# Another model of the chip behind the order of each engine's instructions, in a two-block transformer kernel

## The chip, the cores and the metric

The kernel runs on one core of one Trainium2 chip. The metric is the time of one execution on the device in microseconds (us), as the median of several runs; the other times here come from one execution that the hardware profiler recorded.

## The reference, cut to what matters

The reference is one stack of three layers on a sequence of 512 positions with 1024 features. Everything is computed in 32-bit floats.

```python
def reference(x, ...):
    x = first_block(x, ...)             # attention, HGRN2, RWKV-7 and RG-LRU side by side, then an MLP
    return second_block(x, c_2, ctx_2, ...)   # two layers, with a context of 256 rows

# first_block
h = rms_norm(x, norm_mix_pre)
pa, pb, pc, pd = split(h @ w_in)
mix = concat([chunk_attention(pa), hgrn2(pb), rwkv7(pc), rglru(pd)])
x = x + rms_norm(mix @ w_out, norm_mix_post)
x = x + rms_norm(square(relu(rms_norm(x) @ mlp_w1)) @ mlp_w2, norm_mlp_post)

# second_block, layer l of 2
mx = silu(c) @ ada_w[l] + ada_b[l]       # shifts, scales and gates
hx = rmsnorm(x) * (1 + scale) + shift    # the same for the context rows
yx = mixer_ab(hx, hc) if l == 0 else mixer_mla(hx, hc)   # window + differential / latent attention
x = x + gate * rmsnorm(yx)
x = x + gate * rmsnorm(swiglu(modulated x, ffn_w13[l], ffn_w2[l]))
```

## The kernel before

Every large product is made in three passes of TensorE (`mm3`, L203 to L209): each operand is kept as a high and a low part of a reduced float type, and high x high, low x high and high x low are added in one PSUM bank. A weight comes from HBM into `wr` (L186 and L183, three buffers, from SyncE's queue), ScalarE makes its high part `wh` (L199) and VectorE its low part `wl` (L200), two buffers each. An accumulated bank is emptied by VectorE or ScalarE, in the last products of a block by `out_last` (L1101, the sum at L1115).

The program is one straight line without loops at run time. It is written with Python generators: `weave` (L241) takes one step of a main generator and then, by a share written as a number (`W`, L1864, and `STEP`, L2068), steps of others, so that matmuls of one part stand between the dependent steps of another. In the first block the steps of RWKV (L527 to L592), of HGRN2 (L795 to L870) and of attention are woven with projections and with the `ada` products (L1016, the matmuls at L1028, two buffers of 1024 KB for their tile `aw`, loads at L1026). In layer 0 of the second block a unit of attention computes its scores while the one before it is weighted (`unit`, in `mixer0`, L2075); layer 1 does the same for latent attention (`Mla`, L1553). Between blocks stands a chain for each pair of 128-row tiles (`Post`, L1802): a product with a gain row (L1825 on GpSimd, L1826 on VectorE), a sum of squares (ScalarE, L1848), a power on GpSimd (L1852), the residual (L1829), the same norm again with L1837 at its end, and transposes on TensorE (L1754 in `two_to_F`) whose results become the next block's operands.

The order of the program is not the order of the engines. When the context of the kernel closes, a scheduler goes through all instructions with a model of the chip: at each moment of the model's time an engine gets, among the instructions whose inputs and buffers the model holds to be ready, the one that stands first in the program. What comes out is one fixed list for each engine, with semaphore waits, and the engines work through their lists.

## Time and profile before

| | us |
|---|---|
| median of 3 runs | 2566.88 |
| lowest, highest | 2566.58, 2567.56 |
| the profiled execution | 2560.58 |
| its span, first to last instruction | 2558.5 |
| TensorE busy in it | 2440.3 |
| VectorE, ScalarE, GpSimd busy | 1203.4, 995.0, 303.7 |

The profiled execution is 6.3 us shorter than the median. A matmul counts as busy from its start to a modelled end, so a row of matmuls without a hole is busy all the time, whatever their pace. In the rows below PE is TensorE's matmuls and PEld its weight loads, DVE is VectorE, ACT ScalarE, POOL GpSimd and SPq the queue of SyncE; L12 is line 12 of the kernel. PEclk is the granted share of TensorE's full clock.

### The profile page before, as it was taken

The page shows a single profiled execution, that of the slowest core. Times are in us where ns is not written, and L with a number is a line of the kernel's source. Part 1 is how long each engine was busy: PE and PEld are TensorE (multiplying, and loading weights), DVE is VectorE, ACT ScalarE, POOL GpSimd, SP SyncE. Part 2 cuts the span into 40 slices and gives each one's busy share as a digit, 9 for nine tenths or more (in the row PEclk, how much of TensorE's full clock was granted, in tenths as well). Part 3 has the DMA queues.
Part 4 walks back from the last instruction along what each step waited for, and adds up shares of the span by engine and source line. Part 5 has one row for each costly group of instructions (what it writes and reads, how often), then busy time and mean ns, then how long its engine had stood idle before and what let it go on. Part 6 is the DMA issues. An engine that isn't in the chain of part 4 may idle for free. (4 is left out here: it accounts for less than half of the span.)

```text
span 2558.5 us, 37902 instructions
## 1 busy us (share of the span) xinstructions
PE 2440.3 (95%) x15436; PEld 1976.2 (77%) x15436; DVE 1203.4 (47%) x2075; ACT 995.0 (39%) x1802; POOL 303.7 (12%) x393
## 2 busy tenths in 40 slices
PE   8999989999999989989899999999899999999998
PEld 6567747888888867767888888888776667888886
DVE  5644464433446575773531232333656663523334
ACT  4742234332235454653522221212555554432222
POOL 0101132000001122320200000000222221000001
PEclk9999999999999999999999999999999999999999
DMA  8754575333334312122412222222321123333332
GB/s 267 258 197 163 167 267 167 91 91 99 93 105 139 85 45 66 56 84 83 148 58 66 59 66 66 73 68 71 112 60 35 40 66 117 114 93 97 99 107 91
DMA packets 251005, 270.74 MB, mean 106 GB/s; under 512 B 23744, under 2 KB 198256, under 8 KB 244688
## 3 DMA queue, kind: packets, MB, share of 16 engines
q1 hardware_dynamic: 249600, 264.00, 33.4%
q0 software_dynamic: 1232, 4.33, 0.5%
q8 instruction: 121, 1.98, 0.3%
q14 instruction: 52, 0.43, 0.0%
HBM read 231.90 MB, written 25.45 MB: 101 GB/s over the span
## 5 line engine op out<-in xcount | busy, mean ns | idle before, releaser
L207 PE MATMUL ps<-hFh,wh 128*128 128x512 f32 (+1 forms) x1752 | 628.8, 360 | 7.8 <-ACT qk_l L1273 2.5
L208 PE MATMUL ps<-hFl,wh 128*128 128x512 f32 (+1 forms) x1752 | 624.9, 357 | 1.8 <-DVE hFl L266 1.6
L209 PE MATMUL ps<-hFh,wl 128*128 128x512 f32 (+1 forms) x1752 | 623.3, 356 | 0.5 <-DVE wl L200 0.5
L200 DVE TENSOR_TENSOR wl<-wr,wh 128x1024 fp32r<-128x1024 f32 (+3 forms) x258 | 307.0, 1191 | 651.5 <-ACT wh L199 649.5
L199 ACT CAST wh<-wr 128x1024 fp32r<-128x1024 f32 (+3 forms) x258 | 263.1, 1021 | 704.2 <-PE ps L208 346.5
L207 PEld LDWEIGHTS ps<-hFh,wh 128*128 128x128 f32 x1752 | 333.4, 191 | 72.9 <-issue 12.1
L209 PEld LDWEIGHTS ps<-hFh,wl 128*128 128x128 f32 x1752 | 333.4, 191 | 52.0 <-issue 4.3
L208 PEld LDWEIGHTS ps<-hFl,wh 128*128 128x128 f32 x1752 | 333.8, 191 | 48.9 <-DVE hFl L266 3.2
L207 PE MATMUL ps<-wh,h_h 128*128 128x512 f32 x590 | 229.7, 389 | 0.6 <-ACT wh L199 0.6
L208 PE MATMUL ps<-wl,h_h 128*128 128x512 f32 x590 | 229.7, 389 | 0.0
L209 PE MATMUL ps<-wh,h_l 128*128 128x512 f32 x590 | 229.5, 389 | 0.0
L1825 POOL TENSOR_TENSOR yg<-y,gainrow 128x512 f32<-128x512 f32 x28 | 38.7, 1384 | 1319.6 <-DVE y L1115 866.7
L207 PEld LDWEIGHTS ps<-wh,h_h 128*128 128x128 f32 x590 | 110.8, 188 | 24.0 <-ACT wh L199 1.1
L208 PEld LDWEIGHTS ps<-wl,h_h 128*128 128x128 f32 x590 | 110.8, 188 | 22.9 <-DVE wl L200 0.2
L209 PEld LDWEIGHTS ps<-wh,h_l 128*128 128x128 f32 x590 | 110.8, 188 | 23.0
L1234 DVE TENSOR_TENSOR hraw<-hraw,ps 128x512 f32<-128x512 f32 (+1 forms) x70 | 40.1, 573 | 174.4 <-PE ps L209 174.4
L265 ACT CAST h_h<-hraw 128x512 fp32r<-128x512 f32 (+1 forms) x70 | 36.9, 527 | 120.9 <-DVE hraw L1234 120.9
L208 PE MATMUL ps<-wl,hFh 128*128 128x256 f32 (+2 forms) x256 | 80.3, 314 | 0.2 <-DVE wl L200 0.2
L207 PE MATMUL ps<-wh,hFh 128*128 128x256 f32 (+2 forms) x256 | 80.4, 316 | 0.1
L209 PE MATMUL ps<-wh,hFl 128*128 128x256 f32 (+2 forms) x256 | 80.0, 312 | 0.0
L1626 DVE TENSOR_REDUCE sm<-ps 128x1 f32<-128x768 f32 x64 | 60.8, 954 | 37.4 <-PE ps L209 36.2
L1630 POOL TENSOR_SCALAR ms<-ms,sm 128x768 f32<-128x768 f32 x64 | 60.2, 943 | 150.2 <-DVE sm L1629 145.3
(643 smaller groups left out, 4197.9 us busy)
## 6 DMA issues: line engine op xcount, KB each, us to landing
wr<-in_ffn_w_dram SPq DMA_DIRECT2D x126, 512.0 KB, 3.9
aw<-in_ada_w_dram SPq DMA_DIRECT2D x48, 1024.0 KB, 5.1
wr<-in_mlp_w_dram SPq DMA_DIRECT2D x60, 512.0 KB, 4.0
wr<-in_w_in_dram SPq DMA_DIRECT2D x25, 512.0 KB, 6.7
x<-xr SPq DMA_DIRECT2D x20, 512.0 KB, 3.0
xr<-x SPq DMA_DIRECT2D x18, 512.0 KB, 4.4
wr<-in_ab_w_in_dram SPq DMA_DIRECT2D x16, 512.0 KB, 5.0
wr<-in_w_out_dram SPq DMA_DIRECT2D x8, 512.0 KB
```

The source lines that it names most:

```text
L199: nc.scalar.copy(dst(hi), view(raw))
L200: nc.vector.tensor_tensor(out=dst(lo), in0=view(raw), in1=dst(hi).bitcast(F32), op=SUB)
L207: mm(out, a.hi, b.hi, start=start, stop=False)
L208: mm(out, a.hi, b.lo, start=False, stop=False)
L209: mm(out, a.lo, b.hi, start=False, stop=stop)
L265: nc.scalar.copy(s.hi, x)
L1234: v.tensor_tensor(out=raw[:, c], in0=raw[:, c], in1=p, op=MUL)
L1626: v.tensor_reduce(out=mx, in_=p[:, 0:768], axis=AX.X, op=MAX, negate=True)
L1630: nc.gpsimd.tensor_scalar(out=s, in0=s, scalar1=r, scalar2=1.0, op0=MUL, op1=MUL)
L1825: nc.gpsimd.tensor_tensor(out=t[:, h[0]], in0=y[:, h[0]], in1=g[:, h[0]], op=MUL)
```

## The change

The scheduler gets another model of the chip: a model made of timelines in place of the one that executes the program. The one line in `kernel`:

```diff
-    with tile.TileContext(nc) as tc, ExitStack() as es:
+    with tile.TileContext(nc, schedule_with_timeline_sim=True) as tc, ExitStack() as es:
         network(make(tc, I, es), out[0])
```

The instructions, the tiles and the order of the program stay as they are. The five lists, of TensorE, VectorE, ScalarE, GpSimd and SyncE, are made anew, and with them the waits and the buffers that each tile gets.

## Rows read from the trace of the kernel before

**Rows 1.** The page's busy time by engine, and the core's span and clock.
```profile
PE 2440.3 (95%) x15436; PEld 1976.2 (77%) x15436; DVE 1203.4 (47%) x2075; ACT 995.0 (39%) x1802; POOL 303.7 (12%) x393
...
core 0: 2558.5 us, clock 0.984
```
**Rows 2.** Busy us in stretches: PE, PEld, DVE, ACT, POOL; PEclk, DMA share, GB/s.
```profile
0.00:64.00 64.00, 52.14 (x280) 41.12 (x280) 32.29 (x84) 28.52 (x44) 6.06 (x26) 1.00 0.85 267
...
128.00:192.00 64.00, 61.62 (x880) 44.23 (x879) 30.74 (x41) 27.07 (x39) 0.44 (x1) 0.97 0.59 197
192.00:256.00 64.00, 62.55 (x1028) 49.13 (x1028) 30.55 (x51) 16.17 (x26) 7.33 (x4) 1.00 0.50 163
256.00:320.00 64.00, 61.41 (x993) 47.41 (x991) 31.46 (x62) 16.89 (x28) 7.97 (x7) 1.00 0.51 167
320.00:384.00 64.00, 53.93 (x652) 32.12 (x651) 43.00 (x121) 24.99 (x58) 21.70 (x26) 0.95 0.77 267
...
512.00:576.00 64.00, 64.00 (x280) 52.12 (x279) 22.60 (x24) 23.53 (x32) 0.00 (x0) 1.00 0.32 91
...
896.00:960.00 64.00, 56.46 (x313) 42.98 (x310) 45.67 (x100) 35.47 (x74) 17.65 (x27) 0.94 0.17 45
960.00:1024.00 64.00, 59.19 (x361) 48.03 (x362) 35.12 (x99) 29.59 (x69) 16.69 (x29) 0.93 0.23 65
1024.00:1088.00 64.00, 60.53 (x383) 47.71 (x382) 47.89 (x121) 39.40 (x87) 20.63 (x34) 1.00 0.19 58
1088.00:1152.00 64.00, 53.36 (x293) 39.31 (x291) 44.92 (x111) 35.75 (x75) 18.41 (x30) 0.92 0.27 82
...
1856.00:1920.00 64.00, 57.96 (x342) 47.35 (x340) 38.30 (x70) 37.32 (x76) 19.06 (x24) 0.97 0.26 59
1920.00:1984.00 64.00, 62.97 (x386) 44.06 (x385) 39.35 (x66) 34.52 (x70) 17.54 (x18) 1.00 0.14 35
1984.00:2048.00 64.00, 61.93 (x378) 44.13 (x378) 38.85 (x65) 34.22 (x69) 16.60 (x17) 1.00 0.15 41
2048.00:2112.00 64.00, 61.44 (x361) 42.30 (x359) 42.57 (x70) 37.68 (x73) 17.23 (x17) 1.00 0.21 65
...
2496.00:2558.00 62.00, 53.39 (x233) 43.14 (x232) 26.71 (x40) 15.52 (x30) 7.36 (x8) 0.96 0.29 94
```
**Rows 3.** Instructions from 362 to 373: start, duration, what; brackets: idle before, releaser.
```profile
368.93 0.69 DVE L866 TENSOR_TENSOR f<-ps,hsm 128x512 f32<-128x512 f32 x1 [1.54 <-POOL hsm L864]
...
369.68 1.15 PE L869 MATMUL ps<-c_masks,f 64*64 64x64 f32 x32 [1.95 <-DVE f L866]
...
370.76 1.06 PE L1028 MATMUL ps<-aw,sc 128*32 128x512 f32 x8
```
**Rows 4.** The DMA issues of SyncE from 340 to 373, the last two ada loads.
```profile
360.90 5.83 SPq L1026 DMA_DIRECT2D aw<-in_ada_w_dram  x2
```
**Rows 5.** The page's DMA issues: count, KB each, median us from issue to landing.
```profile
aw<-in_ada_w_dram SPq DMA_DIRECT2D x48, 1024.0 KB, 5.1
...
wr<-in_w_in_dram SPq DMA_DIRECT2D x25, 512.0 KB, 6.7
```
**Rows 6.** Instructions from 1784 to 1800, columns as in rows 3.
```profile
1790.86 0.60 PE L1754 MATMUL ps<-c_ident,y 128*128 128x128 f32 x4
...
1792.23 0.68 DVE L1115 TENSOR_TENSOR y<-y,ps 128x512 f32<-128x512 f32 x1
...
1794.85 0.75 DVE L1837 TENSOR_SCALAR y<-xr,sm 128x1024 f32<-128x1024 f32 x1 [1.47 <-POOL sm L1852]
...
1795.74 2.79 PE L1754 MATMUL ps<-c_ident,y 128*128 128x128 f32 x12 [4.29 <-DVE y L1837]
...
1798.19 0.73 PE L207 MATMUL ps<-h_h,h_h 128*128 128x512 f32 x1
```
**Rows 7.** What TensorE waited for in total: us, times, longest us.
```profile
PE ps L1754 <- DVE y L1837: 13.6, 6, 4.3
```
**Rows 8.** Busy us behind the wait of rows 6, columns as in rows 2.
```profile
1795.00:1800.00 5.00, 4.25 (x19) 3.98 (x20) 4.34 (x9) 3.42 (x7) 0.54 (x1) 0.66 0.38 105
```

## What is to be expected of the change

> **What bounds the kernel now.** I read the granted clock first, then the head of the page, then the busy time of each engine in forty stretches of 64 us, then what TensorE waited for, then the order of single instructions around two of its waits. TensorE is busy for 2440.3 of 2558.5 us, no other engine for half of that [rows 1]. So the kernel is bound by its matmuls, and 118.2 us is all the time in which TensorE does nothing. The change leaves the number and the shapes of the matmuls as they are, so it can only win from these 118.2 us and from the slower clock: the mean granted clock is 0.984 [rows 1], and 1.6% of the span, 41 us, is what that costs at most.
>
> The stretches are of three kinds [rows 2]. In 14 of the 40 (896 us: the MLP and the two FFNs; one row stands for all) TensorE is busy for 64.00 of 64 us. Nothing can be won there. The first stretch has 11.9 us of idle time and the last 8.6 us; both are loads and norms with no other work to do. What is left, 97.7 us, lies in the woven stretches, where the chained steps of one generator are filled with the matmuls of another, and at the boundaries between blocks. The woven ones are 128 to 320 (RWKV steps), 896 to 1152 (window and differential attention) and 1856 to 2112 (latent attention): 11 rows, 704 us, of which TensorE does 185.58 + 229.54 + 244.30 = 659.42 us. In 320 to 384, where a chain has little left to be filled with, it is busy for 53.93 of 64 us, a share of 0.843.
>
> **What the change does, part by part.** It adds and removes no instruction, no tile and no DMA. For each engine the scheduler takes the instructions by the moment at which its model of the chip holds them to be ready, and by their place in the program among those that are. The model is exchanged, so the orders on TensorE, VectorE, ScalarE, GpSimd and in SyncE's DMA queue may all move. The model's own run is before the launch and costs nothing in these times. Four effects count.
>
> *Stalls with ready work behind them (a gain).* At 367.7 the matmul at the head of the queue (L869) waits for VectorE (L866), which itself waits for a GpSimd step (L864), and TensorE stands for 1.95 us. Behind it, at 370.76, are eight ada matmuls that need none of this: their tile's load was issued at 360.90 [rows 3, 4], and with the median of 5.1 us to landing [rows 5] it was there at 366.0. They would have put 1.06 us into the hole. At 1790.86 four transposes run, then TensorE waits 4.29 us for a normalised row (L1837), with twelve more transposes first in the queue. The projection matmuls behind those (L207 at 1798.19) begin a new accumulation, and the bank for it is one that L1115 empties at 1792.23 to 1792.91 [rows 6]; from then to 1795.6, 2.7 us, they could have run. So 1.06 + 2.7 of 1.95 + 4.29 us, 60%, could have been filled by another order. A list scheduler puts a waiting matmul ahead of a ready one only where its model takes the first to be ready sooner than the chip makes it so; both cases are a chain of small VectorE, ScalarE and GpSimd steps that ends later on the chip. The largest wait in total is of the same kind: L1754 behind L1837, 13.6 us [rows 7]. The gain lies between 0 and 60% of 97.7 us, 59 us. I take 24 us, two fifths of it: a model that follows these steps more closely fills some holes, but it has errors of its own, and work that fills one hole is missing from a later one. That the new model is the closer one is not in the trace; it is the step of this sum that I can least show.
>
> [...]
>
> *Chain steps that come to stand behind fill (a loss).* The same scheduler chooses between what a chain needs next and what only fills. A filling matmul that is queued as soon as it is ready, in front of the chain's, delays the chain by its length at every step, and it is missing when the chain runs alone. The trace of before bounds this only from far: nothing at the low end (below nothing is the gain above), and at the high end all 704 woven us fall to the share of the stretch with little fill, 659.42 / 0.843 = 782 us, 78 us more than now. In between, the four attention stretches are made of the same kind of units and differ by what they stand next to: TensorE is busy for 53.36 to 60.53 us in them [rows 2], 7.2 us in 64. I take a tenth of that for each of the 11 woven stretches, 8 us, nearest to the low end because the banks and the two buffers of each kind of tile let only a little fill be brought forward.
>
> *The clock (a gain).* [...]
>
> *DMA order and the other engines.* In the first 64 us the transfers fill 85% of the DMA engines at 267 GB/s [rows 2], and 1024 KB loads of ada_w share the queue with 512 KB loads of w_in [rows 5]. An ada load that goes ahead of a w_in load holds it up by 1024 KB / 267 GB/s = 3.9 us; one that goes behind gives as much back. Between -4 and +12 us for up to three of them; I take 0, since the stretch keeps the program's order where the queue is full. VectorE and ScalarE are busy for 47% and 39% [rows 1], so a weight cast that moves by its own length is hidden by two sets of split weights. In the saturated stretches I take 0; if that cover failed, with a stall of 1 us in each, it would be 14 us.
>
> **The sum.** -24 + 8 - 3 + 0 = -19 us on the profiled execution, whose own time is 2560.58 us, its span and 2.1 us around it: 2541.6 us. That execution lies 6.3 us under the median of the timed runs. The forecast is 2541.6 + 6.3 = 2547.9, 2548 us.
>
> **The rivals.**
> (1) *The chain is starved: slower.* The place is the woven stretches, above all the RWKV steps and the attention pairs. For it: these stretches have only 704 - 659.4 = 44.6 us idle, so their fill is well placed now, and any other order must place it as well. Against: in them some ready work nearly always stands behind a stall. A third of the far end, 26 us, against a fifth less of the holes, 9 us, gives 2567 + 17 = 2584 us; the far end alone gives 2645. It decides once a woven stretch loses more than 24 / 11 = 2.2 us.
> (2) *No difference*, since over a third of the kernel is saturated and swaps among ready matmuls move no end, or since both models give nearly the same order. 2562 to 2572 us. Against: the two stalls above show where the orders must differ if the models do.
> [...]
> [...]
>
> **How the numbers follow.** The forecast's case, a small gain (2520 to 2560), has 0.45; rival (3), below 2520, 0.04; rival (2) 0.17; rival (1) 0.34, of which 0.1 lies over 2605. A difference under 0.2%, 5 us, is about what a measurement of this kernel can't tell from none. So faster has 0.49, same 0.17, slower 0.34. Cases of both signs hold most of the chance, so the range holds both: from 2520 to 2605, with 0.04 and 0.1 left out and a little for errors of the sum. The forecast's own range is 2520 to 2560.
>
> **What would show it.** If the step of the gain is right, TensorE's idle time falls from 118 towards 95 us with its busy time unchanged, the ada matmuls stand ahead of L869 or the projections ahead of the last transposes, and L1754's wait for L1837 shrinks from 13.6 us. If rival (1) is right, the woven stretches end later, their idle time grows past 44.6 us, and the waits in their chains (L549, L815, L1329, L1343) grow. If rival (2) is right, each block begins at the same time after the start as now. The reasons are wrong, whatever the time, if it changes inside the MLP or FFN stretches or if TensorE's busy time moves by over 10 us, since the sum takes both as fixed.

## The result, and the profile of the changed kernel

| | before | after |
|---|---|---|
| median | 2566.73 us (4 runs) | 2602.96 us (4 runs) |
| lowest, highest | 2564.84, 2567.56 | 2600.26, 2605.60 |
| after / before | | 1.0155, 95% interval 1.0129 to 1.0182 |
| the profiled execution | 2560.58 | 2603.79 |
| its span | 2558.5 | 2601.8 |

The changed kernel is 1.55% slower, 40 us. The forecast was 2548 us, faster; the time lies inside the range, but on the other side.

The page of after, answering [rows 1]: busy time by engine, span and clock.

```profile
PE 2452.5 (94%) x15436; PEld 1992.8 (77%) x15436; DVE 1201.6 (46%) x2075; ACT 998.1 (38%) x1805; POOL 312.9 (12%) x393
...
core 0: 2601.8 us, clock 0.967
```

The span is 43.3 us longer: TensorE is idle for 149.3 us where it was 118.2, and busy for 12.2 us more with the same 15436 matmul records. Its granted clock fell from 0.984 to 0.967.

Where the time went shows when the same matmul runs in both traces:

| us from the start | before | after | later by |
|---|---|---|---|
| first of RWKV's transposes (L514) | 135.3 | 160.3 | 25.0 |
| last matmul of RWKV (L657) | 305.3 | 330.2 | 25.0 |
| last matmul of HGRN2 (L869) | 370.6 | 399.6 | 29.0 |
| first evacuation of the MLP (L1161) | 444.6 | 482.6 | 38.0 |
| first window scores of layer 0 (L1329) | 879.5 | 912.5 | 33.0 |
| last weighing of layer 0 (L1343) | 1163.8 | 1207.9 | 44.1 |
| last gate of the first FFN (L1234) | 1773.9 | 1818.4 | 44.5 |
| end | 2558.5 | 2601.8 | 43.3 |

So the loss is made in two places, some 33 us in the mixers of the first block and some 11 us in layer 0's attention. Through the MLP and both FFNs the distance stays within 5 us. The table has one execution of each: in the trace of e1 below, which has the lists of before, the first window scores (L1329) come at 885.2 us, 5.7 later than in before.

L514 is not the first matmul of RWKV's chunks. Their product L527 starts at 122.9 us in before and at 133.7 in after, 10.8 us later. L514 takes a bank that, by the semaphore it waits for, ScalarE empties first for the gates of RG-LRU (L900). ScalarE, before and after:

```profile
134.54 0.69 ACT L900 ACTIVATE fw<-ps,c_cols 128x512 f32<-128x512 f32 x1 [4.33 <-PE ps L899]
```

```profile
158.46 0.67 ACT L900 ACTIVATE f<-ps,c_cols 128x512 f32<-128x512 f32 x1
```

In before L514 starts as soon as that is done. RG-LRU's own chain is late on ScalarE: its first step there (L890) runs at 118.27 us in before and at 132.38 in after, where ScalarE works without a gap from 117.3 to 133.4 us and has RWKV's late exponential (L484, at 127.92 instead of 104.83) ahead of it. So the 25 us at L514 pass through the steps of two chains.

Stretches of 64 us of after, columns as in [rows 2].

```profile
64.00:128.00 64.00, 58.53 (x259) 33.35 (x260) 27.69 (x39) 35.19 (x43) 1.53 (x2) 0.95 0.67 225
128.00:192.00 64.00, 54.65 (x555) 35.05 (x549) 40.86 (x57) 36.28 (x47) 9.95 (x5) 0.92 0.63 219
320.00:384.00 64.00, 45.76 (x540) 34.09 (x540) 40.81 (x78) 20.74 (x40) 16.27 (x17) 0.64 0.62 223
512.00:576.00 64.00, 64.00 (x281) 52.59 (x281) 18.14 (x19) 20.84 (x27) 0.00 (x0) 1.00 0.34 99
```

A saturated stretch (512 to 576) is as full as before. From 128 to 192 TensorE is busy for 54.65 us where it was 61.62, and from 320 to 384 for 45.76 where it was 53.93, there at a granted clock of 0.64 where it was 0.95. The same 224 records of L815 in that stretch take 13.5 us where they took 8.8, 313 ns of one in place of 234; in after they run from 353 to 383 us at a granted clock of 0.50, in before from 328 to 353 at 0.94. Before and after (count | busy us, mean ns | idle before, and what ended it):

```profile
L815 PE MATMUL ps<-f,f 64*64 64x64 f32 x224 | 8.8, 234 | 2.6 <-DVE f L811 1.8 <-POOL f L812 0.8
```

```profile
L815 PE MATMUL ps<-f,f 64*64 64x64 f32 x224 | 13.5, 313 | 4.7 <-DVE f L819 2.4 <-POOL f L812 1.2 <-DVE hdec L824 1.1
```

What TensorE waited for in after: us in total, times, longest us.

```profile
PE ps L1028 <- DMA aw<-in_ada_w_dram: 17.0, 11, 4.4
...
PE ps L869 <- DVE f L866: 7.3, 1, 7.3
...
PE ps L1754 <- DVE y L1837: 4.3, 3, 2.2
```

The wait of [rows 7], 13.6 us, did shrink to 4.3, as the gain step said. In its place the ada matmuls (L1028) now wait 17.0 us for their loads, a row that this view of before does not have. L869 waits 7.3 us. That is not the wait of [rows 3] but the earlier of its two places, where before waits 0.77 us at 322.23. In after:

```profile
335.78 0.62 ACT L265 CAST mixs_h<-mixs_l 128x512 fp32r<-128x512 f32 x1 [5.52 <-DMA mixs_l<-dmix]
336.30 0.59 ACT L860 ACTIVATE f<-ps 128x512 f32<-128x512 f32 x1
...
341.98 1.30 PE L869 MATMUL ps<-c_masks,f 64*64 64x64 f32 x19 [7.31 <-DVE f L866]
```

In ScalarE's list a cast (L265) that stands 5.52 us for a DMA is ahead of the chain's step L860, whose matmuls (L857) had ended at 332.8 us and on which L862, L864, L866 and then L869 depend. From 340 to 384 us the granted clock is 0.50.

A chain step of RWKV in both kernels: VectorE ends the operand (L471), TensorE multiplies it (L473). Start, duration, what. Before:

```profile
90.45 0.75 DVE L471 SCALAR_TENSOR_TENSOR f<-f,c_cols,f 128x512 f32<-128x512 f32 x1
...
91.25 1.12 PE L473 MATMUL ps<-f,c_masks 128*128 128x512 f32 x2 [0.56 <-DVE f L471]
```

After:

```profile
104.92 0.75 DVE L471 SCALAR_TENSOR_TENSOR f<-f,c_cols,f 128x512 f32<-128x512 f32 x1
...
105.71 0.40 PE L207 MATMUL ps<-hFh,wh 128*128 128x512 f32 x1
...
109.80 0.40 PE L207 MATMUL ps<-hFh,wh 128*128 128x512 f32 x1
110.03 1.02 PE L473 MATMUL ps<-f,c_masks 128*128 128x512 f32 x2
```

Before, TensorE waits for the step and takes it at once. After, it does not wait: the operand is there at 105.67, and 19 projection matmuls stand in front, 4.36 us. The second L473 starts 4.89 us after the end of its operand (121.27) in after and 0.22 us in before; the first L438 starts 2.95 us after it in after and 0.15 us in before. (The expectation of e10 has two sums over the way to L514, 31 and 12 us; the traces' views do not give them, and nothing here rests on them.) That is the start of the explanation; what it costs had to be measured.

### The profile page after: what moved, and what is told of

Its sections match the earlier page's. It is cut to its first block, busy times and chain, and to the rows that moved or that the text cites. A ratio compares the mean times of both kernels' runs of the same rounds, so it can differ in the third digit from the quotient of the medians.

```text
span 2601.8 us, 37962 instructions
## 1 busy us (share of the span) xinstructions
PE 2452.5 (94%) x15436; PEld 1992.8 (77%) x15436; DVE 1201.6 (46%) x2075; ACT 998.1 (38%) x1805; POOL 312.9 (12%) x393
## 4 chain that ended last, share of the span: by engine, by line
PE 78%; DVE 6%; ACT 3%; DMA 3%; issue 2%; POOL 1%; SPq 0%; DVEq 0%; ACTq 0%; POOLq 0%
PE ps L207 22%; PE ps L208 22%; PE ps L209 22%; PE ps L712 3%; PE ps L697 3%; DMA aw<-in_ada_w_dram 1%; PE ps L1329 1%; PE ps L1028 1%; PE ps L1330 1%; DMA kl<-kl 1%; DVE wl L200 1%; ACT wh L199 1%; DVE hFl L266 0%; DVE sm L1501 0%; PE ps L1343 0%
## 5 line engine op out<-in xcount | busy, mean ns | idle before, releaser
L207 PE MATMUL ps<-hFh,wh 128*128 128x512 f32 (+1 forms) x1752 | 627.6, 360 | 12.2 <-ACT qk_l L1273 7.7
L200 DVE TENSOR_TENSOR wl<-wr,wh 128x1024 fp32r<-128x1024 f32 (+3 forms) x258 | 308.6, 1197 | 715.5 <-ACT wh L199 703.4
L199 ACT CAST wh<-wr 128x1024 fp32r<-128x1024 f32 (+3 forms) x258 | 263.0, 1020 | 720.2 <-PE ps L208 378.7
L207 PEld LDWEIGHTS ps<-hFh,wh 128*128 128x128 f32 x1752 | 334.2, 192 | 76.1 <-issue 12.7
L207 PE MATMUL ps<-wh,h_h 128*128 128x512 f32 x590 | 210.7, 389 | 0.0
L207 PEld LDWEIGHTS ps<-wh,h_h 128*128 128x128 f32 x590 | 110.8, 188 | 23.3 <-DVE y L1069 0.2
L1234 DVE TENSOR_TENSOR hraw<-hraw,ps 128x512 f32<-128x512 f32 (+1 forms) x70 | 40.1, 573 | 177.1 <-PE ps L209 175.2
L265 ACT CAST h_h<-hraw 128x512 fp32r<-128x512 f32 (+1 forms) x70 | 37.0, 528 | 119.5 <-DVE hraw L1234 119.5
L1028 PE MATMUL ps<-aw,sc 128*32 128x512 f32 x384 | 63.6, 685 | 17.0 <-DMA aw<-in_ada_w_dram 17.0
L207 PE MATMUL ps<-wh,hFh 128*128 128x256 f32 (+2 forms) x256 | 78.8, 318 | 0.0
```

The costliest lines, as they stand in the source:

```text
L199: nc.scalar.copy(dst(hi), view(raw))
L200: nc.vector.tensor_tensor(out=dst(lo), in0=view(raw), in1=dst(hi).bitcast(F32), op=SUB)
L207: mm(out, a.hi, b.hi, start=start, stop=False)
L265: nc.scalar.copy(s.hi, x)
L1028: nc.tensor.matmul(p[32 * j:32 * j + 32], K.sc[:, k], raw[:, 512 * j:512 * j + 512], start=k == 0, stop=k == 7)
L1234: v.tensor_tensor(out=raw[:, c], in0=raw[:, c], in1=p, op=MUL)
```

## Experiments

All but e7 and e8 change only the lists, by one method. The program is traced once with the model of before, to read the five lists; then it is traced again, and chosen neighbours of those lists are joined by edges that carry order and no semaphore wait. What no edge holds, the model is free to place.

```diff
+            edge = mybir.DependencyInfo(mybir.DependencyClass.NoSync, mybir.DependencyReason.DATA)
+            for order in lists(made, K.cut):
+                for a, b in zip(order, order[1:]):
+                    tc.add_manual_dep(made[b], names[a], edge, reason="list")
...
+    def lists(made, cut):
+        for e in (E.PE, E.DVE, E.Activation, E.Pool, E.SP):
+            yield [k for k in done if made[k].engine == e]
```

Here `done` is the order of before, and `cut` is the place in the program behind the first block's mixers. The diffs below show only what differs from this. Times are medians; "over" is the ratio to before, run beside it on the same chip, less 1, times 2566.7 us, with its 95% interval in square brackets. On that scale after is 40 us over [33 to 47].

### Which lists, and where

**e1: all five lists of before under the new model** (the code above).

> The new model schedules, but the five engine lists of the kernel before are laid on it as orders without a wait. The computation is unchanged. This is the control for the runs in which only a part of the lists is laid on: if the change acts through the five lists alone, it gives the time of before, 2567 us (2562 to 2572). If something besides the lists moves with the model (the buffer that a tile gets, other semaphore waits), it stays slower, above 2575 us.

Measured: 2561.6 us beside 2562.5, 0.9993 [0.9980 to 1.0006]. The change acts through the lists alone.

**e2, e3 and e18: the lists of before for a part of the program.**

```diff
-            yield [k for k in done if made[k].engine == e]
+            yield [k for k in done if made[k].engine == e and k < cut]      # e2
+            yield [k for k in done if made[k].engine == e and k >= cut]     # e3
+            yield [k for k in done if made[k].engine == e and k < end]      # e18, end: behind mixer0
```

> The lists of before are laid on the new model for the mixers of the first block alone (all that is traced before its last product, some 435 us of the run); the rest keeps the new lists. The computation is unchanged. Theory 1 (the loss is made in the first block, by ada loads and ada matmuls that the new model puts too early, and is +34 us when the MLP begins): 2603 - 34 = 2569 us, with 9 us at most left at the end of layer 0's attention, so 2567 to 2577. Theory 2 (rival 1 as forecast: every woven stretch loses some at its chains, the attention of layer 0 and 1 as much as the first block): half of the 36 us or more stays, over 2585 us.

> The reverse: new lists in the mixers of the first block, the lists of before in everything behind them. The computation is unchanged. Theory 1: 2567 + 34 = 2601 us, at most 9 us under it, so 2592 to 2603; the milestones up to the MLP are those of the changed kernel. Theory 2: under 2585 us, since the attention stretches are those of before again.

> The lists of before in everything up to the end of layer 0's attention (some 1200 us of the run), the new model's lists behind it: both FFNs, latent attention and the boundaries. The computation is unchanged. If the 16 us behind the first block lie in layer 0's attention, as a comparison at equal work says (12 of them between 1050 and 1150 us): 0 to 6 us over before. If they are spread over all that follows: 10 us or more over before.

| | us | ratio to before | over, us |
|---|---|---|---|
| e2: new lists behind the first block | 2579.1 | 1.0064 [1.0044 to 1.0085] | 16 |
| e3: new lists in the first block | 2584.4 | 1.0089 [1.0066 to 1.0113] | 23 |
| e18: new lists behind layer 0's attention | 2564.6 | 1.0015 [1.0002 to 1.0029] | 4 |

e2 and e3 add up to 39 us, the whole loss, so the two parts do not depend on each other as far as intervals of some 6 us each can tell. The first block makes 23 us [17 to 29], layer 0 with the MLP ahead of it 16 - 4 = 12, give or take 6, all the rest 4 [1 to 7]. In the traces some 10 of the 12 us lie in layer 0: from its first L1329 to its last L1343 it takes 284.3 us in before and 283.1 in e1, 295.4 in after and 293.6 in e2. e18 ends where its first case said. e2 and e3 both end between the numbers of the two theories: the first block has the larger part, but not 34 us of it.

**e4 and e5: lists of before for some engines only.**

```diff
-        for e in (E.PE, E.DVE, E.Activation, E.Pool, E.SP):
+        for e in (E.PE,):                                  # e4
+        for e in (E.DVE, E.Activation, E.Pool, E.SP):      # e5
```

> Only TensorE's list of before is laid on the new model; VectorE, ScalarE, GpSimd and the DMA queue of SyncE are ordered by the new model around it. The computation is unchanged. Theory 1a (what hurts is the place of the ada matmuls in TensorE's in-order queue): 2567 to 2575 us, and the waits of L1028 for aw, 17.0 us in the changed kernel, fall under 3 us. Theory 1b (what hurts is the DMA queue, an ada load of 1024 KB ahead of a w_in load, which no order of TensorE mends unless the loads follow it): over 2585 us, with new waits of L207 for weights. Theory 2 (chains on VectorE and ScalarE stand behind other steps in their own queues): over 2585 us too, but with waits of TensorE for VectorE in the woven stretches.

> The reverse of the run with only TensorE's list of before, which gave 2627 us: VectorE, ScalarE, GpSimd and SyncE keep the lists of before, and the new model orders TensorE around them. The computation is unchanged. Theory 1 (each engine's list is right only together with the others'): slower than before, over 2580, since the matmuls still come by the new model's times. Theory 2 (the late steps are in the queues of VectorE and ScalarE, and TensorE's own order matters little): 2563 to 2575 us, with the waits in the attention stretches those of before.

Measured: e4 2627.1 us, 1.0254 [1.0234 to 1.0274]; e5 2687.2 us, 1.0482 [1.0465 to 1.0499]. Each half of before's lists beside the other half of the new ones is slower than either whole. In e4 the waits of L1028 for aw are gone, as theory 1a said, and L514 is back at 142.5 us, but the time that it named is missed by far: HGRN2 ends at 394.6 (before 370.6), and layer 0's attention takes 314.4 us, 30 more than in before. e5 is the case of its theory 1. So neither TensorE's list nor the other four carry the loss by themselves: a list is good or bad with the others.

### The ada loads

**e7 and e8: ada loads of a quarter, under the new lists and under those of before.**

```diff
-            nc.sync.dma_start(out=raw, in_=w[:, k, 2048 * s:2048 * s + 2048])
+            nc.sync.dma_start(out=raw[:, 0:512], in_=w[:, k, 2048 * s:2048 * s + 512])
             for j in range(4):
-                nc.tensor.matmul(p[32 * j:32 * j + 32], K.sc[:, k], raw[:, 512 * j:512 * j + 512], ...)
+                nc.tensor.matmul(p[32 * j:32 * j + 32], K.sc[:, k], raw[:, 0:512], ...)
```

> The five lists of the changed kernel are kept, but each ada load brings only its first 256 of 1024 KB, and its four matmuls all read that quarter (so the modulation of the second block, and with it the output, differs); number, shape and order of all instructions stay. Theory 1 (in the first block TensorE stands for ada data, 17.0 us, and the slow clock behind those waits costs as much again as half of it): the waits of L1028 for aw go, and the time falls by 17 to 25 us to 2578 to 2586. Theory 2 (those waits only cover steps of the chains that would end late anyway): the waits go to RWKV and HGRN2 rows and the time falls by under 8 us, over 2595.

> The same quarter loads under the five lists of the kernel before (the output differs in the same way): the control for what smaller ada loads give besides, to other loads of the first block. Theory 1: before waits for no ada data, so at most 5 us, 2558 to 2566, and the difference to the quarter loads under the new lists is 17 to 25 us where it was 40. Theory 2: also near 2563, but the difference stays at 32 us or more.

Measured: e7 2593.0 us, 1.0112 [1.0090 to 1.0134], 29 over; e8 2559.4 us, 0.9995 [0.9983 to 1.0007]. The ada data cost the new lists 11 us (1.0155 - 1.0112, give or take 9) and those of before nothing that can be told. That is between the theories: 11 us, and some 30 stay.

**e9: the ada work not ahead of its place in before's lists.**

```diff
+        for e in (E.PE, E.SP):
+            order = [k for k in done if made[k].engine == e]
+            yield from ([a, b] for a, b in zip(order, order[1:]) if b in adas)
```

> The new model schedules all, with one kind of edge more: no ada load and no ada matmul may stand in its engine's list ahead of the instruction that stood just before it in the list of before. The computation is unchanged. Theory 1 (the early ada work is the whole loss of the first block): the first RWKV matmul L514 is back from 160 to under 142 us, and the time falls by about the 22 us that the new lists of the first block cost alone, to 2577 to 2585. Theory 2 (the first block loses at its chains, whatever the ada work does): over 2595 us, with the waits on other rows.

Measured: 2610.5 us, 1.0181 [1.0161 to 1.0202]: no gain. What TensorE waited for in e9 from 60 to 200 us (one line is added to the file, so L1029 is L1028):

```profile
PE ps L207 <- ACT fw L758: 7.3, 1, 7.3
PE ps L549 <- DVE rL L533: 5.5, 1, 5.5
PE ps L207 <- DVE f L738: 3.0, 1, 3.0
PE ps L1029 <- DMA aw<-in_ada_w_dram: 1.5, 2, 1.3
```

The 9.9 us that after waits there for aw are down to 1.5, and 15.8 us of waits for ScalarE and VectorE stand in their place. Two of them are the fill's own: a projection (L207) waits until ScalarE (L758) or VectorE (L738) has emptied its bank. Theory 1 falls: the ada work moved back by itself wins nothing.

### Chain steps behind fill

**e10 and e11: chain steps not behind fill that before had behind them**, on TensorE alone and on all engines.

```diff
+        def step(k):
+            return k < cut and made[k].debug.bass_funcname.startswith(
+                ("Rwkv", "Lru", "Hgrn.run", "Hgrn.feed_f", "Ctx.rsqrt_wide"))
+
+        for e in (E.PE,):                                            # e10; all five in e11
+            order = [k for k in done if made[k].engine == e]
+            for n, (a, b) in enumerate(zip(order, order[1:])):
+                if step(a) and not step(b):
+                    yield from ([a, c] for c in order[n + 1:n + 61] if not step(c))
```

> The new model schedules all, with edges of one kind: in the mixers of the first block, a matmul of RWKV, RG-LRU or HGRN2 that before had in TensorE's list ahead of filling matmuls (projections, ada, attention) stays ahead of the next sixty list entries of before that are no such step. The other four lists are free. The computation is unchanged. Theory 3 (the steps of the chains stand ready behind fill in TensorE's in-order queue; in the changed kernel this is 31 us of the way from 40 us to the first RWKV matmul, before 12): L514 is back from 160 to 150 us or earlier, and the time falls by 10 to 22 us, to 2581 to 2593. Rival (the new lists of VectorE, ScalarE and SyncE hold the chains up as well, as the run with TensorE's list alone suggests): L514 comes back, but HGRN2's end at L869 stays at 390 us or later and the time stays over 2595.

> The same edges on all five engines: the chains' own steps (RWKV, RG-LRU, HGRN2, with their loads) are not put behind what before had behind them; fill and attention stay free on every engine. The computation is unchanged. Theory 3: nearly all of the 22 us that the first block's new lists cost goes: 2578 to 2588, with L514 under 145 and L869 under 382 us. Rival (the loss lies in the order of the fill itself, ada before projections, so that fill is missing later, whatever the chains do): over 2595.

Measured: e10 2601.1 us, 1.0152 [1.0126 to 1.0177], 39 over; e11 2591.7 us, 1.0118 [1.0101 to 1.0136], 30 over. In e10 L514 is back at 145.2 us, but HGRN2 ends at 392.1 and the time is that of after, as the rival said. With all engines some 10 us of the 40 come back, give or take 8. That lies between the two cases of e11, and L514 (146.4 us) and L869 (389.4) miss the places that theory 3 named. The steps' places matter, on all engines together; they are not the whole of it.

**e12, e19 and e14: eight entries of before's TensorE list moved.**

```diff
+        order, late, fill = [], [], 0
+        for k in (k for k in done if made[k].engine == E.PE):
+            f = made[k].debug.bass_funcname
+            if f in ("Rwkv.gates", "Rwkv.norms", "Rwkv.features"):
+                late.append((fill + 24, k))        # e19: 12
+                continue
+            order.append(k)
+            fill += f == "Ctx.mm3"
+            while late and late[0][0] == fill:
+                order.append(late.pop(0)[1])
+        yield order
```

In e12 and e19 the other four lists are held to those of before; in e14 they are not, and the model of before makes them.

> The lists of before on all engines, but in TensorE's list eight of its entries, the matmuls of RWKV's gates, norms and features (L438, L452, L473), each stand 24 projection matmuls later: one projection bank, some 5.4 us by the 0.23 us of one. Nothing else moves. The computation is unchanged. Theory 3 (a chain step behind fill delays the chain by the length of that fill, and the fill is missing when the chain runs): L514 goes from 136 to 140 us or later and the time rises by 3 to 6 us. Rival (TensorE does the same work in another order, so nothing is lost as long as some fill is left): within 2 us of before.

> The lists of before on all engines, with the same eight matmuls (L438, L452, L473) 12 instead of 24 projection matmuls later in TensorE's list: half a bank, some 2.7 us. The computation is unchanged. If the delay is multiplied (theory 4: some 20 us for a whole bank): 8 to 12 us over before, and L514 some 8 to 12 us later. If it comes at once with the first missed turn: 16 us or more. If the half bank is absorbed: under 4 us.

> The same eight matmuls (L438, L452, L473) stand 24 projection matmuls later in TensorE's list of before, but the other four lists are not held to those of before: the model of before makes them anew around TensorE's list, so weight casts and bank evacuations may go ahead of the steps that now come later. The computation is unchanged. Theory 4 (the in-order lists of ScalarE and VectorE multiply the delay: the casts L199 and L200 for the projections stand behind the late chain step, so the fill itself stops and the next step is late again): the 20 us of the run with all lists held shrink to 2 to 9 us, and the waits of L207 for L199 and of L209 for L200 (5.9 and 5.2 us between 60 and 160 us) go. Rival (the delay itself is the cost: RWKV starts late and the fill that ran instead is missing later): 15 us or more over before, as with all lists held.

| | us | ratio to before | over, us | L514 at |
|---|---|---|---|---|
| e12: 24 later | 2580.8 | 1.0087 [1.0070 to 1.0105] | 22 | 158.4 |
| e19: 12 later | 2565.4 | 1.0015 [1.0003 to 1.0026] | 4 | 142.9 |
| e14: 24 later, other lists free | 2574.7 | 1.0048 [1.0028 to 1.0067] | 12 | 147.0 |

Eight matmuls of TensorE's list, one projection bank later, cost 22 us [18 to 27]: four times the 5.4 us of the bank (the estimate in e12's expectation; in after 19 such matmuls took 4.36 us), over both cases of e12, and as much as the new lists cost in the whole first block. L514 starts at 158.4 us, in after at 160.3. How 5.4 becomes 22 shows in the timelines of e12, of ScalarE, VectorE and TensorE (brackets: idle before, and what ended it):

```profile
110.62 0.63 ACT L484 ACTIVATE f<-f 128x512 f32<-128x512 f32 x1 [16.99 <-DVE f L483]
...
115.80 1.03 ACT L199 CAST wh<-wr 128x1024 fp32r<-128x1024 f32 x1
```

```profile
109.23 0.69 DVE L475 TENSOR_TENSOR rbonus<-ps,rvl 128x512 f32<-128x512 f32 x1 [10.63 <-PE ps L473]
...
118.63 1.20 DVE L200 TENSOR_TENSOR wl<-wr,wh 128x1024 fp32r<-128x1024 f32 x1
```

```profile
108.18 1.02 PE L473 MATMUL ps<-f,c_masks 128*128 128x512 f32 x2
116.88 0.50 PE L207 MATMUL ps<-hFh,wh 128*128 128x512 f32 x1 [3.69 <-ACT wh L199]
119.88 0.79 PE L209 MATMUL ps<-hFh,wl 128*128 128x512 f32 x1 [2.27 <-DVE wl L200]
```

L473 runs at 108.18 instead of 91.25. VectorE holds the next step (L475) at the head of its list and stands for 10.63 us; ScalarE stands for 16.99 us at the step behind that. Behind both in the lists are the casts L199 and L200 of the next projection's weight. The last load of such a weight ahead of them was issued at 96.27 us, and the cast L199 runs at 115.80. So the fill stops too: TensorE waits 3.69 us for the one and 2.27 us for the other, and the next chain matmul, which stands behind that fill, is later again: the groups of L438, L452 and the two of L473 start 6.9, 8.4, 16.9 and 24.3 us later than in before. The same holds for a chain of which no matmul was moved: RG-LRU's L890 on ScalarE goes from 118.27 to 141.09 us. In e14 the waits of TensorE for the casts are all but gone (0.3 us from 60 to 160 us) and 10 of the 22 us come back, give or take 7; there a new wait of 7.9 us stands at L207 for L758, a bank that ScalarE empties behind a late step. That is between the two cases of e14: about half of the cost hangs on how the other engines' lists are laid, and what makes the rest is not shown. Half the dose costs 4 us [1 to 7], less than half of 22: the cost grows faster than the delay. It ends where e19 called the half bank absorbed, though L514 is still 7.6 us late.

e12 shows what late steps can cost; after is not e12. From 60 to 200 us TensorE waits in after for none of these casts, but 9.9 us for ada data.

### Layer 0's attention

In e2 (lists of before in the first block), VectorE from 1069 to 1083 us:

```profile
1070.42 0.69 DVE L257 TENSOR_TENSOR pt_l<-ps,pt_h 128x512 fp32r<-128x512 f32 x1 [0.43 <-ACT pt_h L256]
...
1078.29 1.23 DVE L200 TENSOR_TENSOR wl<-wr,wh 128x1024 fp32r<-128x1024 f32 x1 [2.42 <-ACT wh L199]
...
1081.44 0.69 DVE L1541 TENSOR_TENSOR pt_h<-ps,sm 128x512 f32<-128x512 f32 x1 [1.13 <-POOL sm L1013]
1082.05 0.41 DVE L1501 TENSOR_REDUCE sm<-ps 128x1 f32<-128x256 f32 x1
```

The maximum of a differential unit's scores (L1501) runs at 1082.05; its matmul had ended at 1066.1. It stands 15.9 us behind the norm of the unit before it (L1541) and what that waits for.

**e15: on VectorE the scores' steps not behind what before had behind them**, with e2's lists in the first block.

```diff
+        order = [k for k in done if made[k].engine == E.DVE]
+        for n, (a, b) in enumerate(zip(order, order[1:])):
+            if step(a) and not step(b):          # step: Win.scores, Diff.scores
+                yield from ([a, c] for c in order[n + 1:n + 61] if not step(c))
```

> The lists of before in the mixers of the first block, as in the run that gave 1.0064 of before (16 us), and behind it the new model with one kind of edge: on VectorE a step of the scores (the maxima L1419 and L1501 and what belongs to them) stays ahead of the next sixty list entries of before that are no such step. The computation is unchanged. Theory 4 in layer 0 (the maximum of one unit's scores stands up to 16 us behind the norm at the end of the other unit's weighing, L1541, in VectorE's list): L1343 ends at 1172 us or earlier where it was 1180, and the time is 2 to 8 us over before. Rival (TensorE's list or ScalarE's makes that loss): 12 us or more over before.

Measured: 2590.5 us, 1.0114 [1.0088 to 1.0140]: 29 over, 13 more than e2, and the last L1343 at 1195.9 us, so theory 4 fails here. That is the rival's range, but no run shows the rival's cause. One engine's list pulled towards before makes it worse, as in e4 and e5. What costs layer 0's 12 us is not settled.

### The gain term, and a version that might beat both

**e16 and e17: ready matmuls put into TensorE's holes.** The lists of before; from the trace of before a table names matmuls that were ready, with their banks, while TensorE waited, and they are put ahead of the waiting one.

```diff
+        order = [k for k in done if made[k].engine == E.PE]
+        ahead = {at: who for at, who in MOVES}          # e16: 98 entries at 25 places; e17: 30 at 7
+        moved = {i for _, who in MOVES for i in who}
+        yield [order[j] for i in range(len(order)) if i not in moved for j in (*ahead.get(i, ()), i)]
```

> The lists of before on all engines, but in TensorE's list 98 matmuls stand further ahead, in 25 of its waits of before that were 0.5 us or longer: by the times of the trace of before each was ready, with its bank and its operands, when that wait began or before it ended, and together they take 17.5 us. The largest pieces are 2.35 us of projections ahead of the twelve transposes at 1795.7, 2.17 us at 808 and 1.47 us of ada at 158.8. The computation is unchanged. The gain term of the forecast (a hole that ready matmuls fill is won; 24 us were taken): 12 to 18 us under before, 2544 to 2551. Rival (the work that fills one hole is missing from a later one, or holds up what the other lists wait for): less than 5 us, or slower.

> The lists of before with only those of the 25 filled waits that lie next to a saturated stretch or in layer 0's attention: 30 matmuls of TensorE's list, 6.7 us, stand further ahead, most of them before the transposes at 808 and 1795.7 us. The computation is unchanged. If a filled hole pays where saturated work follows (the run with all 25 was 7 us ahead of before at 1800 us and gave 4 of them back later): 4 to 8 us under before. If it is given back all the same: within 3 us of before.

Measured: e16 2556.3 us, 0.9987 [0.9975 to 1.0000], 3 us under (0 to 6) for 17.5 us of filled holes; e17 2563.8 us, 1.0002 [0.9989 to 1.0015]. Both are the second case of their expectations. Where it went shows in e17 at the hole of [rows 6], which it fills with 2.35 us of projections. TensorE's waits and the transposes there, in before behind the four of 1790.86 [rows 6]:

```profile
1795.74 2.79 PE L1754 MATMUL ps<-c_ident,y 128*128 128x128 f32 x12 [4.29 <-DVE y L1837]
...
1813.81 1.50 PE L1754 MATMUL ps<-c_ident,y 128*128 128x128 f32 x12 [1.45 <-DVE y L1837]
```

In e17:

```profile
1796.21 0.60 PE L1754 MATMUL ps<-c_ident,y 128*128 128x128 f32 x4
1798.72 0.50 PE L207 MATMUL ps<-h_h,h_h 128*128 128x512 f32 x1 [1.91 <-DVE y L1115]
...
1801.52 1.50 PE L1754 MATMUL ps<-c_ident,y 128*128 128x128 f32 x12 [0.47 <-DVE y L1837]
...
1813.40 0.50 PE L207 MATMUL ps<-h_h,h_h 128*128 128x512 f32 x1 [1.00 <-DVE y L1115]
...
1819.19 2.79 PE L1754 MATMUL ps<-c_ident,y 128*128 128x128 f32 x12 [3.23 <-DVE y L1837]
```

The wait of 4.29 us shrinks to 1.91 us, in which the filling matmuls' own bank is still being emptied (L1115), and 0.47 us. At the next pair of tiles the wait of 1.45 us becomes 1.00 and 3.23 us. The second twelve transposes start 22.95 us behind the first four in before and 22.98 us in e17, so the filled hole won nothing: in that stretch the boundary's chain sets the pace, and work put in early is missing in front of its next step. TensorE is busy for 61.82 us from 1785 to 1855 in before, and for 61.88 us from 1791 to 1861 in e17.

**e13: new lists from the second block's latent attention alone**, where e2, 16 us behind before at the end of the first FFN, had come to some 10 us behind it.

```diff
-            yield [k for k in done if made[k].engine == e]
+            yield [k for k in done if made[k].engine == e and (k < start or k >= end)]   # around layer 1's latent attention
```

> The lists of before everywhere except for what is traced between the second block's first FFN and the end of its latent attention (some 1800 to 2190 us of the run), where the new model's lists are free. The computation is unchanged. There the run with before's lists in the first block alone fell from 16 to 10 us behind before: the wait of L1754 for L1837 shrinks from 13.6 to about 4 us. If that gain stands by itself: 3 to 7 us under before. If it only came from projections that the pinned neighbours now hold back: within 2 us of before.

Measured: 2569.0 us, 1.0036 [1.0022 to 1.0049], 9 us slower, outside both. The wait of L1754 for L1837 stays at 13.6 us. Layer 1's first transposes at L1742 start 16.5 us earlier than in before, and the second FFN, where before's lists are held again, 7.7 us later. In e2 the gain did not last either: at the first gate of the second FFN (L1234) it is 15.6 us behind before. None of these versions beats before by what can be told.

## Why the prediction was wrong, point by point

- **What bounds the kernel**: right. Saturated stretches did not change, and the loss is idle time and clock in the woven ones, the RWKV steps and layer 0's attention; latent attention, also named, adds next to nothing (e18).
- **TensorE's busy time is fixed**: wrong by 12.2 us, more than the 10 us that the prediction allowed. The matmuls are the same; the clock they ran at was not, 0.967 in the mean where it was 0.984, and one of L815 takes 313 ns at 0.50 where it took 234 at 0.94.
- **Stalls filled, -24 us**: the step that gave the sign, and it failed. The new order does fill holes: L1754's wait falls from 13.6 to 4.3 us. But TensorE's idle time rose from 118.2 to 149.3 us where the prediction had it fall, and a filled hole is not time won: e16 put 17.5 us of ready work into 25 holes and won 3 us (0 to 6), e17 6.7 us and won none that can be told. The prediction's bound (what was ready while TensorE stood) counted the work and not the next wait of the same chain. That the new model is the closer one, which the prediction called the step it could least show, no run shows; its lists are the slower ones.
- **Chain steps behind fill, +8 us**: the mechanism occurs, as L473 shows with 4.36 us behind 19 projection matmuls, and its size was far too small. It was taken from how four attention stretches differ, 0.7 us in each of 11. The first block alone loses 23 us and layer 0 some 12; how much of that is this mechanism is not shown, but one bank ahead of eight matmuls can cost 22 us (e12). What was left out is that VectorE and ScalarE have lists too, in which the fill's casts and evacuations stand behind the chain's steps. The prediction took a moved cast as hidden by two sets of split weights; in e12 TensorE waits 3.69 and 2.27 us for the casts all the same. The cast L199 runs there at 115.80 us, behind a step of ScalarE that had waited 16.99 us. The prediction had no term for work that stands behind a late step in the lists of these engines.
- **DMA order, 0 us between -4 and +12**: the ada data cost 11 us by e7 against after, near the far end of the range, but not in the way that the term named. It priced loads that go ahead of one another in the first 64 us; of the 17.0 us that ada matmuls wait for their data, 2.4 lie there. The order of SyncE's list did move (its first two ada loads are issued at 15.7 us, in before the first at 22.0), but whether the loads or the matmuls that read them stand in the wrong place, no run separates: e9 moved both.
- **The clock, -3 us**: no run shows this term of the sum, what a spell of slow clock costs and how many go; in before the clock is 0.66 over the 5 us of [rows 8]. Its sign was wrong too: the mean fell from 0.984 to 0.967. From 320 to 384 us, where TensorE is idle for 18 us, the granted clock is 0.64, and it is 0.50 from 340 us on, behind the wait of 7.31 us; that it falls behind idle time is how the rows stand, no run here separates the two.
- **Rival (1), the chain is starved, 2584 us**: its sign and two of its places, the RWKV steps and layer 0's attention, are what happened, at 2603 us. Its point of decision, 2.2 us in each woven stretch, was the wrong measure: the loss is not spread but sits where few steps are late. Of the waits that it named, L1329's for L1419 grew from 1.2 to 6.0 us, while L1343's for L1509 fell from 8.8 to 2.8; where L473 is late behind fill, its operand there at 105.67 us and the matmul at 110.03, TensorE shows no wait at all. Rival (2) and rival (3), a time below 2520 us, fell with it: the steps of the table begin 25 to 45 us later, and the holes were not won.

What is shown: the lists are the whole cause (e1), with 23 us in the first block, 12 in layer 0 and the MLP, 4 behind (e2, e3, e18); the ada data cost 11 us (e7, e8); a few late chain steps can cost 22 (e12), some 10 of them by how the other engines' lists are laid (e14). Not shown: that late chain steps are what costs after its time, and how they and the ada data share the first block's 23 us, since e9 and e10 each took one away and the time stayed; what makes the 12 us of layer 0; and why the new model places the steps as it does.

## What to carry to other kernels

A schedule is one object over all engines: price a moved step not by its own length but by what stands behind it in the lists of the engines that its result feeds, above all the fill's own casts and evacuations; in e12 eight matmuls moved by some 5.4 us cost 22 us. A hole in the busiest engine, even with ready work behind it, need not be worth its length: here 3 of 17.5 us came out, and where the chain that ends the hole set the pace, in e17, none. And look for late chain steps where an engine does not wait: compare when the operand ended with when its reader ran.

## What the runs showed that was not expected

- Eight matmuls 24 projection matmuls later cost 22 us, 12 later 4 us.
- In e1 the same lists give times that go with the granted clock: four executions had 2556.1 to 2557.4 us at 0.985 to 0.987, and three 2563.5 to 2564.5 us at 0.980 to 0.983. In the four of after they do not: the longest, 2605.6 us, has the highest clock, 0.973.
- Lists of two schedules mixed by engine are slower than both, by 65 us (e4) and 124 us (e5) over before.
